# An encoder whose 1/rms row reaches the partitions through DRAM instead of through TensorE transposes

## The chip, the cores and the metric

The kernel runs on one core of a Trainium2 chip. The metric is the device time of one launch in microseconds (us); one launch computes the whole encoder. PE stands for the matrix engine, DVE, ACT and POOL for the vector, scalar and GpSimd engines, SP for the queue that starts most of the loads.

## The reference

The input x is 512 tokens by 1024 features, in fp32. There are two layers of this kind, and a final norm:

```python
for l in range(2):
    h = rms_norm(x, norm_g[l, 0])
    x = x + 0.5 * swiglu(h, ...)                    # 1024 -> 2816 -> 1024
    h = rms_norm(x, norm_g[l, 1])
    ya = neighbourhood_attention(h, ...)            # 8 heads of 64
    yb = diff_attention(h, ...)                     # 4 heads of 2 x 64, values of 128
    yc = window_gqa(h, ...)                         # 8 heads of 64
    g = sigmoid(h @ w_gate[l] + b_gate[l])          # a gate for each of the three branches
    x = x + (sum of g_i * (branch_i @ w_branch[l, i])) @ w_o[l]
    h = rms_norm(x, norm_g[l, 2])
    x = x + 0.5 * swiglu(h, ...)
return rms_norm(x, final_g)

def rms_norm(x, g):
    return x * lax.rsqrt(jnp.mean(x * x, axis=-1, keepdims=True) + EPS) * g
```

A differential head forms two softmax maps, takes one minus lambda times the other, multiplies the values by this, and then has an rms norm of its own over the 128 features of its output for each token. So each layer has three norms of x that go through the code in question, and four head norms: six and eight in the whole kernel. (The final norm is computed in another way.)

## The kernel before

**Tiling.** x is kept transposed: 8 tiles of 128 features (partitions) by 512 tokens. A product of the weights with h gives a tile of 128 output features by 512 tokens. fp32 precision comes from a split of both factors into a high and a low part; `product` (L97, L98, L100) issues 24 matmuls for one output tile where the inner size is 1024: for each of 8 chunks high by high and high by low, then 8 times low by high. The value projections (L492, L493, L495) have the tokens as output partitions instead. The weights come from DRAM once (`weights`: L82 a DMA on SP's queue, L83 a cast on ACT, L84 a subtraction on DVE).

**The norms.** The gain is folded into h; the factor 1/rms of each token is applied after the products. `sums` (through `rstd`) makes four small matmuls with a column of ones (L157, two records each in the trace), which give the sum of squares for 4 x 128 tokens as four columns in the PSUM tile `st`; DVE scales them and adds epsilon (L158), POOL raises them to -0.5 (L159). The result `rs` has tokens on partitions. The value products, whose outputs have tokens on partitions, use it as it is (`vn<-mm,rs`). Everything else needs one row of 512 factors repeated on all 128 partitions: `spread` (L165) makes four PE transposes of a broadcast column into `st`, and in `finish` ACT copies the tile to SBUF as `rb` (L150). The first user of `rb` is a DVE multiplication that reads a product in PSUM: `gn` (L296) in a feed-forward part, `qn` (L451) in a mixer. There are three PSUM buffers for products (`mm`), one for `st`, two for scores (`s`), one for transposed maps (`t`), one for a head's output (`av`).

**Where the six norms stand.** In a feed-forward part, `sums` comes behind the first product of the part and `finish` behind the second. In a mixer, `sums` comes behind the query product, `finish` behind the key product, and two value products of 24 half-width matmuls follow. The first feed-forward part of layer 0 (`opening`) runs four products at once while x and weights come in; its 32 low-part matmuls (L353) come last, with `sums` behind the 16th and `finish` behind the 24th.

**The differential heads.** `attend_diff` is a generator that gives its work in 8 pieces (two maps for each of four blocks of 128 queries); `beside` takes one piece, then issues some side products (gates, query and key products of later heads, merges), and what a piece leaves for later is issued one step (one piece) behind: scores and softmax (L533, L534, L544, L547), then the transposes of the map (L672 on PE, `ph` on ACT by L673, `pl` on DVE by L674), then the gather (L689), then for a whole head the sum of squares (`rstd_of`), then `scaled`: four transposes of the factors (L165 again), one DVE instruction that reads them from PSUM (L705), and the split of the head's output into `yp` (ACT L107, DVE L109), which the merges read much later. A head's norm thus falls into the first pieces of the next head. The third head's falls into the fourth, the fourth's into the first grouped-query pair.

**What sets the order.** The instructions of each engine are put in order by the tile framework's scheduler from its own estimates; on the chip each engine runs its list in order, and waits where something isn't there. POOL issues the DMAs that keep x in DRAM (`d_x`, L61), read it back (`x`, L56) and swap the halves of query tiles (`qks`, L464, L465), and in a mixer it forms the position bias tiles `nab` (L617).

Of the kernel before, what the change touches and what calls it, by code (L numbers as in the profile page):

```python
# [11 lines left out]
F32 = mybir.dt.float32  # L12
# [4 lines left out]
P = 128  # L17
# [16 lines left out]
def encoder(ctx: ExitStack, tc: tile.TileContext, a: dict, out: bass.AP):  # L34
# [77 lines left out]
    class Norm:  # L112
# [27 lines left out]
        def sums(self):  # L140
# [3 lines left out]
            rstd(self.acc, 1.0 / D, rt, self.rs)  # L144

        def finish(self):

            pb = spread(self.rs)
            rb = work.tile([P, S], F32, tag="rb", name="rb", bufs=1)
            nc.scalar.copy(rb, pb)  # L150
            self.rb = rb

# [7 lines left out]

    def spread(rs):

        pb = st_tile()
        for j in range(4):
            nc.tensor.transpose(pb[:, j * P : (j + 1) * P], rs[:, j : j + 1].to_broadcast([P, P]), ident)  # L165
        return pb

# [83 lines left out]
    def ffn(l, i, h, nxt=None):  # L251
        with tc.tile_pool(name="ffn", bufs=1) as fp:
# [5 lines left out]
            for m in range(2 if first else 0, MF):  # L258
                wg = weights(a["w_gu"][l, i, m, 0])
                wu = weights(a["w_gu"][l, i, m, 1])  # L260
                pg = mm_tile()
                product(pg, cols(wg, KC), h.hi, h.lo)
                if m == 0:
                    h.sums()
                pu = mm_tile()
                product(pu, cols(wu, KC), h.hi, h.lo)
                if m == 0:
                    h.finish()
                if m == 4 and first:
                    position_tables()  # L270
                    small_values()
                if nxt is None and 4 <= m < 4 + KC:
                    if m == 4:
                        xt = fp.tile([P, 4, D], F32, tag="xt", name="xt")
                    x_turned(xt, m - 4)
                gated(h, fp, pg, pu, ghi, glo)
# [28 lines left out]
    def opening(l, i, h, fp, ghi, glo):  # L305
# [42 lines left out]
        for k in range(KC):  # L348
            h.square(k, xs[k])
        for n in range(4):  # L350
            for k in range(KC):
                wk = slice(k * P, (k + 1) * P)
                nc.tensor.matmul(ps[n], ws[n][1][:, wk], h.hi[k], start=False, stop=k == KC - 1)  # L353
            if n == 1:
                h.sums()
            if n == 2:
                h.finish()
        gated(h, fp, ps[0], ps[1], ghi, glo)
# [71 lines left out]
    def mixer(l, h, nxt):  # L430
        with tc.tile_pool(name="mix", bufs=1) as mp:
# [36 lines left out]
            def qk(n):  # L468

                pq = projected(2 * n)  # L470
                if n == 0:
                    h.sums()
                    pk = projected(1)
                    h.finish()
                q = scaled_by(pq, -0.125)
# [183 lines left out]
            def attend_diff(head):  # L659
# [38 lines left out]
                def rstd_of(o, sq):  # L698
                    rt = small.tile([P, 8], F32, tag="rt", name="rt", bufs=3)
                    rstd(sq, 1.0 / P, rt, rt)  # L700
                    return lambda: scaled(o, rt)

                def scaled(o, rt):
                    pb = spread(rt)
                    nc.vector.scalar_tensor_tensor(out=o, in0=o, scalar=sg, in1=pb, op0=ALU.mult, op1=ALU.mult)  # L705
                    ys[1].append(split(o, mp, "yp", 12))
# [178 lines left out]
            beside(attend_diff(1), [g0(5)[0], merge(0, 2), qk(6), v_diff(1)], 6)  # L885
            beside(attend_diff(2), [*g0(6, 7), merge(0, 3), qk(7)], 5)
            beside(attend_diff(3), [gqa_keys(), gqa_queries(0), *g1(0, 1, 2)], 6)
            beside(attend_gqa(0), [*[gqa_queries(p) for p in (1, 2, 3)], merge(1, 0), *g1(3, 4)], 6)
            beside(attend_gqa(1), [merge(1, 1), *g1(5, 6), merge(1, 2), *g1(7)], 5)
            beside(attend_gqa(2), [merge(1, 3), *[gate(2, m, "v", 8) for m in range(3)]], 4)  # L890
# [112 lines left out]
```

## Time and profile before

| | |
|---|---|
| median of 3 runs | 2495.88 us (2495.48 to 2496.05) |
| the profiled execution's own time | 2496.59 us |
| its span | 2494.8 us |
| mean granted TensorE clock | 0.999 |
| PE busy | 2469.8 us |
| DVE, ACT, POOL busy | 1352.6, 983.4, 188.8 us |

The page of the profile covers one execution. Its rows give an engine's instruction group as "line, engine, operation, output from inputs, shape, count", with the busy time and the mean duration; a timeline row begins with the start in us from the start of the span and the duration in us, and ends, in brackets, with the idle time of the engine ahead of it and what ended that. The ends of matmuls are modelled: the spacing of their starts is a better measure than their duration.

### The profile page before, as it was taken

What the parts mean: (1) busy time and instruction counts of PE and PEld (TensorE: products, weight loads), DVE (VectorE), ACT (ScalarE), POOL (GpSimd) and SP (SyncE); (2) the same over time, 40 slices, a digit from 0 to 9 for tenths busy, and PEclk for the clock granted to TensorE, in tenths of its full rate; (3) what the DMA queues carried; (4) which work ended last, traced back from release to release, by engine and by line L of the source; (5) the groups of instructions that cost most, each with busy time, mean ns of one, the idle gap of its engine ahead of it and who ended that gap; (6) DMA issues with size and microseconds to landing.
All of it is one profiled execution on the core that took longest, in us unless ns stands there. A gap on an engine that the chain in (4) does not pass through costs nothing. (4 is left out here: it accounts for less than half of the span.)

```text
span 2494.8 us, 30423 instructions
## 1 busy us (share of the span) xinstructions
PE 2469.8 (99%) x11800; PEld 2059.5 (83%) x11800; DVE 1352.6 (54%) x2331; ACT 983.4 (39%) x1608; POOL 188.8 (8%) x287
## 2 busy tenths in 40 slices
PE   8999999999999999999999999999999999999998
PEld 6788888888888788888888888888888888888887
DVE  5444336876777644443344443377776777444432
ACT  4332224644555433332233332256445554333222
POOL 1000003311000000000000000032110001000000
PEclk9999999999999999999999999999999999999999
DMA  5333444432322342324433234443322224333232
GB/s 162 100 101 91 120 135 128 113 93 84 99 86 79 120 131 94 100 91 125 131 104 99 94 96 128 141 122 104 94 87 90 89 74 148 124 113 97 93 101 68
DMA packets 80271, 265.24 MB, mean 106 GB/s; under 512 B 10720, under 2 KB 15360, under 8 KB 80128
## 3 DMA queue, kind: packets, MB, share of 16 engines
q1 hardware_dynamic: 67968, 228.42, 29.7%
q0 software_dynamic: 11008, 33.03, 4.6%
q8 instruction: 93, 1.52, 0.3%
q10 hardware_dynamic: 1152, 1.86, 0.2%
q14 instruction: 50, 0.41, 0.1%
HBM read 241.22 MB, written 12.62 MB: 102 GB/s over the span
## 5 line engine op out<-in xcount | busy, mean ns | idle before, releaser
L97 PE MATMUL mm<-h,whi 128*128 128x512 f32 x2112 | 829.1, 393 | 0.0
L98 PE MATMUL mm<-l,whi 128*128 128x512 f32 x2112 | 826.4, 391 | 0.0
L83 ACT CAST whi<-raw 128x1024 fp32r<-128x1024 f32 (+1 forms) x414 | 430.4, 1042 | 782.6 <-PE mm L98 363.7
L84 DVE TENSOR_TENSOR wlo<-raw,whi 128x1024 fp32r<-128x1024 f32 (+1 forms) x414 | 499.6, 1207 | 285.2 <-ACT whi L83 158.7
L100 PE MATMUL mm<-h,wlo 128*128 128x512 f32 x2112 | 522.0, 389 | 0.0
L100 PEld LDWEIGHTS mm<-h,wlo 128*128 128x128 f32 x2112 | 396.3, 188 | 82.6
L97 PEld LDWEIGHTS mm<-h,whi 128*128 128x128 f32 x2112 | 396.8, 188 | 81.0 <-issue 2.2
L98 PEld LDWEIGHTS mm<-l,whi 128*128 128x128 f32 x2112 | 396.7, 188 | 79.0
L299 DVE TENSOR_TENSOR un<-mm,rb 128x512 f32<-128x512 f32 x87 | 60.1, 691 | 296.7 <-PE mm L100 296.7
L288 PE MATMUL mm<-g,whi 128*128 128x512 f32 x528 | 205.4, 389 | 0.0
L289 PE MATMUL mm<-g,whi 128*128 128x512 f32 x528 | 205.4, 389 | 0.0
L107 ACT CAST g<-un 128x512 fp32r<-128x512 f32 x88 | 54.7, 622 | 250.5 <-DVE un L300 250.5
L296 DVE TENSOR_TENSOR gn<-mm,rb 128x512 f32<-128x512 f32 x88 | 60.8, 691 | 133.6 <-PE mm L100 133.6
L291 PE MATMUL mm<-g,wlo 128*128 128x512 f32 x528 | 131.4, 389 | 0.0
L547 ACT ACTIVATE lg<-lg,negm 128x256 f32<-128x256 f32 (+1 forms) x192 | 114.6, 597 | 29.7 <-DVE negm L544 28.0
L61 POOL DMA_DIRECT2D d_x<-x x40 | 22.1, 553 | 1249.7 <-DVE x L247 1249.4
L288 PEld LDWEIGHTS mm<-g,whi 128*128 128x128 f32 x528 | 99.1, 188 | 20.6
L291 PEld LDWEIGHTS mm<-g,wlo 128*128 128x128 f32 x528 | 99.1, 188 | 20.6
L289 PEld LDWEIGHTS mm<-g,whi 128*128 128x128 f32 x528 | 99.1, 188 | 20.6
L297 ACT ACTIVATE gn<-gn 128x512 f32<-128x512 f32 x88 | 56.0, 636 | 123.9 <-DVE gn L296 123.9
L109 DVE TENSOR_TENSOR g<-un,g 128x512 fp32r<-128x512 f32 x88 | 60.9, 692 | 62.2 <-ACT g L107 62.2
L247 DVE SCALAR_TENSOR_TENSOR x<-mm,x 128x512 f32<-128x512 f32 x40 | 27.7, 692 | 109.5 <-PE mm L291 72.7
(214 smaller groups left out, 3048.2 us busy)
## 6 DMA issues: line engine op xcount, KB each, us to landing
raw<-in_w_gu SPq DMA_DIRECT2D x172, 512.0 KB, 3.5
raw<-in_w_down SPq DMA_DIRECT2D x48, 512.0 KB, 3.6
raw<-in_w_gate SPq DMA_DIRECT2D x48, 512.0 KB, 3.6
raw<-in_w_qk SPq DMA_DIRECT2D x44, 512.0 KB, 3.6
raw<-in_w_branch SPq DMA_DIRECT2D x24, 512.0 KB, 3.6
raw<-in_w_last SPq DMA_DIRECT2D x22, 512.0 KB, 3.5
d_x<-x POOLq DMA_DIRECT2D x40, 256.0 KB, 2.5
x<-d_x POOLq DMA_DIRECT2D x40, 256.0 KB, 2.9
```

What stands on the lines that cost most here:

```text
L83: nc.scalar.copy(hi[:, w], raw[:, w])
L84: nc.vector.tensor_tensor(out=lo[:, w], in0=raw[:, w], in1=f(hi[:, w]), op=ALU.subtract)
L97: nc.tensor.matmul(ps, wh, xhi[k], start=k == 0, stop=False)
L98: nc.tensor.matmul(ps, wh, xlo[k], start=False, stop=False)
L100: nc.tensor.matmul(ps, wl, xhi[k], start=False, stop=k == n - 1)
L109: nc.vector.tensor_tensor(out=lo, in0=src, in1=f(hi), op=ALU.subtract)
L288: nc.tensor.matmul(ps, w[k][0], ghi[c + k], start=c + k == 0, stop=False)
L289: nc.tensor.matmul(ps, w[k][0], glo[c + k], start=False, stop=False)
L291: nc.tensor.matmul(ps, w[k][1], ghi[c + k], start=False, stop=c + k == MF - 1)
L296: nc.vector.tensor_tensor(out=gn, in0=pg, in1=h.rb, op=ALU.mult)
L299: nc.vector.tensor_tensor(out=un, in0=pu, in1=h.rb, op=ALU.mult)
L547: nc.scalar.activation(p, p, AF.Exp, bias=negm, scale=-1.0, accum_out=total)
```

## The change

`spread` no longer uses PE. It writes the 4 x 128 factors as a row of 512 numbers to a tile in DRAM (a POOL DMA, 512 pieces of 4 bytes), and a second POOL DMA reads this row back to all 128 partitions (256 KB). `finish` is gone, and with it ACT's copy; for a norm of x the two DMAs stand directly behind POOL's power, and the tile that they fill is `rb`. In `opening`, `sums` stands ahead of the 32 low-part matmuls. For a differential head the row goes to a tile `rd` (one of the two `x` buffers), and `scaled` is issued one step later, by `after(1, ...)`, and reads `rd` from SBUF. Some side products stand beside another piece: the merge that stood beside the third head now stands beside the fourth, and the gates of the second branch move on by one.

```diff
@@ class Norm
             rstd(self.acc, 1.0 / D, rt, self.rs)
-        def finish(self):
-            pb = spread(self.rs)
-            rb = work.tile([P, S], F32, tag="rb", name="rb", bufs=1)
-            nc.scalar.copy(rb, pb)
-            self.rb = rb
+            self.rb = work.tile([P, S], F32, tag="rb", name="rb", bufs=1)
+            spread(self.rs, self.rb, f"d_r{self.step}")
...
-    def spread(rs):
-        pb = st_tile()
-        for j in range(4):
-            nc.tensor.transpose(pb[:, j * P : (j + 1) * P], rs[:, j : j + 1].to_broadcast([P, P]), ident)
-        return pb
+    def spread(rs, rb, name):
+        row = dram.tile([1, S], F32, tag=name, name="d_r")
+        nc.gpsimd.dma_start(at(row, 0, [[1, P], [P, 4]]), rs[:, :4])
+        nc.gpsimd.dma_start(rb, row.to_broadcast([P, S]))
@@ def ffn
                 product(pu, cols(wu, KC), h.hi, h.lo)
-                if m == 0:
-                    h.finish()
@@ def opening
             h.square(k, xs[k])
+        h.sums()
         for n in range(4):
             for k in range(KC):
                 wk = slice(k * P, (k + 1) * P)
                 nc.tensor.matmul(ps[n], ws[n][1][:, wk], h.hi[k], start=False, stop=k == KC - 1)
-            if n == 1:
-                h.sums()
-            if n == 2:
-                h.finish()
@@ def qk
                     pk = projected(1)
-                    h.finish()
@@ def attend_diff
                     rstd(sq, 1.0 / P, rt, rt)
-                    return lambda: scaled(o, rt)
-                def scaled(o, rt):
-                    pb = spread(rt)
+                    pb = work.tile([P, S], F32, tag="x", name="rd", bufs=2)
+                    spread(rt, pb, f"d_r{l}_{head}")
+                    return after(1, lambda: scaled(o, pb))
+                def scaled(o, pb):
                     nc.vector.scalar_tensor_tensor(out=o, in0=o, scalar=sg, in1=pb, op0=ALU.mult, op1=ALU.mult)
@@ the pieces and what is issued beside them
-            beside(attend_diff(2), [*g0(6, 7), merge(0, 3), qk(7)], 5)
-            beside(attend_diff(3), [gqa_keys(), gqa_queries(0), *g1(0, 1, 2)], 6)
-            beside(attend_gqa(0), [*[gqa_queries(p) for p in (1, 2, 3)], merge(1, 0), *g1(3, 4)], 6)
-            beside(attend_gqa(1), [merge(1, 1), *g1(5, 6), merge(1, 2), *g1(7)], 5)
+            beside(attend_diff(2), [*g0(6, 7), qk(7)], 4)
+            beside(attend_diff(3), [merge(0, 3), gqa_keys(), gqa_queries(0), *g1(0, 1)], 6)
+            beside(attend_gqa(0), [*g1(2), *[gqa_queries(p) for p in (1, 2, 3)], merge(1, 0), *g1(3)], 6)
+            beside(attend_gqa(1), [*g1(4), merge(1, 1), *g1(5, 6), merge(1, 2), *g1(7)], 6)
```

The scheduler puts the new instructions into each engine's list. Three places show what came of it.

POOL, at the start of layer 0's mixer, before (`nab` is a piece of position bias, `qks` a half of a swapped query tile):

```order
L61 DMA d_x<-x 128x512
L56 DMA x<-d_x 128x512
L159 TENSOR_TENSOR rs<-rt,nhalf 128x4
L617 TENSOR_TENSOR nab<-mask,rp 128x256 x6
L465 DMA qks<-qk 64x512
L464 DMA qks<-qk 64x512 x2
L465 DMA qks<-qk 64x512
```

and with the change, at the same place:

```order
L154 TENSOR_TENSOR rs<-rt,nhalf 128x4
L159 DMA d_r<-rs 128x4x1
L605 TENSOR_TENSOR nab<-mask,rp 128x256 x3
L160 DMA rb<-d_r 128x512
L605 TENSOR_TENSOR nab<-mask,rp 128x256 x3
L454 DMA qks<-qk 64x512
L453 DMA qks<-qk 64x512 x2
```

The write of the row follows the power at once; three of the six bias pieces stand between it and the issue of the read. Line numbers shift: the power is L159 before and L154 now, the bias L617 and L605.

DVE, where the norm of the second differential head ends, before (`o` is the head's output, `st` the transposed factors):

```order
L544 ISA lg_5140,negm_5080<-s_5137,dpb_5000 128x512
L544 ISA negm_5080 128x1
L705 SCALAR_TENSOR_TENSOR o_5076<-o_5076,sg_256,st_5147 128x512
L84 TENSOR_TENSOR wlo_5374<-raw_5372,whi_5373 128x1024
L730 RECIPROCAL tot_5081<-tot_5081 128x2
L109 TENSOR_TENSOR yp_5155<-o_5076,yp_5153 128x512
```

and with the change:

```order
L722 SCALAR_TENSOR_TENSOR lg_5078<-lg_5078,tot_5074,lg_5103 128x512
L694 SCALAR_TENSOR_TENSOR o_5034<-o_5034,sg_256,rd_5089 128x512
L440 SCALAR_TENSOR_TENSOR qn_5141<-mm_5116,rb_2667 128x512
L532 ISA lg_5162,negm_5157<-s_5159,dpb_4993 128x512
L532 ISA negm_5157 128x1
L109 TENSOR_TENSOR yp_5168<-o_5034,yp_5166 128x512
L448 TENSOR_TENSOR qk_5143<-qn_5141,qk_5143 64x512
L448 TENSOR_TENSOR qk_5146<-qn_5141,qk_5146 64x512
L662 TENSOR_TENSOR pl_4996<-t_5170,ph_4995 128x4x128
```

The scaling (L705 before, L694 now) stands one piece later, and behind it now stand the next softmax (L532) and the low part `pl` of the next transposed map, which the gather reads. On ACT the same place now reads (`yp` is the high part of the scaled output, `ph` that of the transposed map):

```order
L83 CAST whi_5391<-raw_5390 128x1024
L107 CAST yp_5166<-o_5034 128x512
L661 CAST ph_4995<-t_5170 128x4x128
L447 CAST qk_5143<-qn_5141 64x512
```

so that ACT takes the cast of the scaled output ahead of the map's.

DVE, for the third head, with the change:

```order
L694 SCALAR_TENSOR_TENSOR o_5386<-o_5386,sg_256,rd_5456 128x512
L440 SCALAR_TENSOR_TENSOR qn_5508<-mm_5483,rb_2667 128x64x8
L662 TENSOR_TENSOR pl_5303<-t_5460,ph_5302 128x4x128
L532 ISA lg_5523,negm_5518<-s_5520,dpb_5300 128x512
L532 ISA negm_5518 128x1
```

Here the low part of a map (L662) stands behind the scaling too; PE writes the next map into the same PSUM buffer `t` only after it.

## The prediction

> **What bounds the kernel now.** I read the shares of busy time first, then the costliest groups:
>
> ```profile
> PE 2469.8 (99%) x11800; PEld 2059.5 (83%) x11800; DVE 1352.6 (54%) x2331; ACT 983.4 (39%) x1608; POOL 188.8 (8%) x287
> L97 PE MATMUL mm<-h,whi 128*128 128x512 f32 x2112 | 829.1, 393 | 0.0
> ```
>
> PE is busy for 2469.8 of 2494.8 us, and its largest group had 0.0 us of idle time ahead of it. So only two things can move the time: PE instructions that go, and PE idle time that goes or comes. The other engines count where PE waits for them. The transposes that go, with what PE waited for ahead of them:
>
> ```profile
> L165 PE MATMUL st<-ident,rt x32: 271/272/323, 579.5 to 1935.4; 128*128 128x128 f32 x32
> L165 PE MATMUL st<-ident,rs x24: 270/272/306, 34.6 to 2134.8; 128*128 128x128 f32 x24
>   POOL rt L159: 8.8, 12
> ```
>
> These are 8 groups of four for heads (`rt`) and 6 for norms (`rs`). What a group costs is read from the starts around it in the timeline, for the second head of layer 0, which didn't wait, and for the other three:
>
> ```profile
> 28.24 3.79 PE L353 MATMUL mm<-h,wlo 128*128 128x512 f32 x16
> ...
> 578.47 0.39 PE L97 MATMUL mm<-h,whi 128*128 128x512 f32 x1
> 579.50 0.65 PE L165 MATMUL st<-ident,rt 128*128 128x128 f32 x4 [0.64 <-POOL rt L159]
> 579.91 0.48 PE L98 MATMUL mm<-l,whi 128*128 128x512 f32 x1
> ...
> 619.26 0.39 PE L534 MATMUL s<-qk,qks 128*128 128x512 f32 x1
> 619.48 0.60 PE L165 MATMUL st<-ident,rt 128*128 128x128 f32 x4
> 619.84 0.48 PE L97 MATMUL mm<-h,whi 128*128 128x512 f32 x1
> 620.16 0.40 PE L98 MATMUL mm<-l,whi 128*128 128x512 f32 x1
> ...
> 659.62 0.65 PE L165 MATMUL st<-ident,rt 128*128 128x128 f32 x4 [0.73 <-POOL rt L159]
> ...
> 702.10 0.65 PE L165 MATMUL st<-ident,rt 128*128 128x128 f32 x4 [0.18 <-POOL rt L159]
> ```
>
> Matmuls of this width start (3.79 - 0.39) / 15 = 0.2275 us apart (the first row, from the opening). The second head's group moved the next matmul from 619.49 to 619.84, and the one behind it by 0.09 more (0.32 instead of 0.23): 0.45 us. The first head's: 579.91 - 578.47 - 0.23 = 1.21, and 0.09 makes 1.30, or the bracket plus 0.66. By that rule the third costs 1.39 and the fourth 0.84. **Removed** from PE: 1.30 + 0.45 + 1.39 + 0.84 = 4.0 us in a layer, 8.0 in two, and 6 x 0.45 = 2.7 at the norms.
>
> **The new path.** Behind POOL's power now stand two DMAs, one after the other. The nearest rows:
>
> ```profile
> d_x<-x POOLq DMA_DIRECT2D x40, 256.0 KB, 2.5
> x<-d_x POOLq DMA_DIRECT2D x40, 256.0 KB, 2.9
> d_gqa<-tg POOLq DMA_DIRECT2D x1, 16.0 KB, 1.7
> POOL x L56 <- DMA d_x<-x: 96.7, 35, 4.4
> L61 POOL DMA_DIRECT2D d_x<-x x40 | 22.1, 553 | 1249.7 <-DVE x L247 1249.4
> q0 software_dynamic: 11008, 33.03, 4.6%
> ```
>
> A POOL DMA issue takes 0.55 us (553 ns). The kernel has this very pattern already, a write to DRAM and a read of it: POOL waited 96.7 / 35 = 2.76 us behind the issue of the write, so 3.3 us from start to start. I take 3.55 for the 512 pieces of 4 bytes, a quarter more for the many pieces (my choice). The read is like `x<-d_x`, 256 KB to 128 partitions: 0.55 + 2.9 = 3.45. Together 7.0 us from the end of the power to `rb` or `rd`, where a group of transposes took 0.45 us and a copy. Lower bound: both like `d_gqa`, 0.55 + 1.7, with the 0.25 by which the wait of 2.76 is longer than the 2.5 of the row: 2.5 each, 5.0. Upper bound: a piece costs what a packet of that queue takes, 0.046 x 2494.8 x 16 / 11008 = 0.167 us; 512 pieces on 16 engines are 32 x 0.167 = 5.3 us, with 0.55 and `d_gqa`'s 1.7 some 7.5, and 11.0 with the read.
>
> [...]
>
> **The opening.** Rows of before:
>
> ```profile
> 31.87 0.95 PE L157 MATMUL st<-ones,acc 128*128 128x1 f32 x8
> ...
> 33.51 1.04 POOL L159 TENSOR_TENSOR rs<-rt,nhalf 128x4 f32<-128x4 f32 x1 [22.59 <-DVE rt L158]
> ...
> 36.02 0.68 DVE L296 TENSOR_TENSOR gn<-mm,rb 128x512 f32<-128x512 f32 x1
> ...
> 36.94 0.39 PE L97 MATMUL mm<-h,whi 128*128 128x512 f32 x1
> ```
>
> The sums stood at 31.87, 3.63 us behind the first low-part matmul at 28.24, and now stand at 28.24, so the power ends at 34.55 - 3.63 = 30.9, `rb` is there at 37.9, `gn` ends at 38.6. All four product buffers are taken, so the next product can start only then, at 38.7 and not at 36.94: **+1.75**. PE has run out of low-part matmuls by 28.24 + 0.8 + 32 x 0.2275 = 36.3.
>
> **The mixers.** Three of six bias pieces stand on POOL between the two DMAs.
>
> ```profile
> 384.90 1.05 POOL L159 TENSOR_TENSOR rs<-rt,nhalf 128x4 f32<-128x4 f32 x1 [1.85 <-DVE rt L158]
> 388.71 3.21 POOL L617 TENSOR_TENSOR nab<-mask,rp 128x256 f32<-128x256 f32 x3 [2.77 <-DMA rp<-in_na_rpb]
> 391.22 1.28 DVE L451 SCALAR_TENSOR_TENSOR qn<-mm,rb 128x512 f32<-128x512 f32 x2
> 392.96 0.28 PE L492 MATMUL mm<-whi,h 128*128 128x256 f32 x1
> ...
> 1621.92 3.24 POOL L617 TENSOR_TENSOR nab<-mask,rp 128x256 f32<-128x256 f32 x3 [3.02 <-DMA raw<-in_w_v]
> 1625.88 0.28 PE L492 MATMUL mm<-whi,h 128*128 128x256 f32 x1
> ```
>
> The first bias piece waits for its table until 388.71, and three take 3.21. So the read is issued at 391.92, though the row is there by 385.95 + 3.55 = 389.5. `rb` comes at 391.92 + 3.45 = 395.4, `qn` 0.7 later. The query, key and first value products hold the three `mm` buffers; the second value product needs the query's, so it starts at 396.2 instead of 392.96: **+3.25**. In layer 1: 1625.16 + 3.45 + 0.7 + 0.1 = 1629.45 instead of 1625.88: **+3.6**. Both include the transposes that go. A quicker write doesn't shorten these two.
>
> **The other feed-forward parts.** There `gn` frees a buffer for the fourth product. The worst of the three is the last:
>
> ```profile
> 2128.07 0.94 PE L157 MATMUL st<-ones,acc 128*128 128x1 f32 x8
> ...
> 2130.42 1.03 POOL L159 TENSOR_TENSOR rs<-rt,nhalf 128x4 f32<-128x4 f32 x1
> ```
>
> The power ends 3.4 us behind the sums' start, `rb` follows at 10.4, `gn` ends at 11.1. PE needs the buffer 0.94 + 2 x 24 x 0.2275 = 11.85 behind the same start. So two whole products hide it (by 0.75 us here, one for one beyond that; I price the other two by this one), and what stays is **3 x -0.45 = -1.35**.
>
> **The heads.** Layer 0's second and third:
>
> ```profile
> 613.33 0.95 PE L157 MATMUL st<-ones,sqd 128*128 128x1 f32 x8
> 614.56 1.45 POOL L159 TENSOR_TENSOR rt<-rt,nhalf 128x4 f32<-128x4 f32 x1 [12.18 <-DVE rt L158]
> ...
> 656.50 0.94 PE L157 MATMUL st<-ones,sqd 128*128 128x1 f32 x8
> 657.98 1.58 POOL L159 TENSOR_TENSOR rt<-rt,nhalf 128x4 f32<-128x4 f32 x1 [10.63 <-DVE rt L158]
> ```
>
> I count from the start of the sums. Second head: the power ends at +2.7, `rd` is there at +9.7, DVE scales it by +10.45, ACT's cast of it ends at +11.1 (0.61) and only then casts the next map's `ph`, by +11.65. PE reaches the gather that needs that map after the sums (0.95), two groups of transposes (0.45 each), three pairs of scores (0.46 each), a product of 24 (5.46) and two matmuls, at +9.15: it idles **2.5**. Third head: power +3.06, `rd` +10.06, scaled +10.8, `qn` (1.05) +11.85, `pl` (0.7) +12.55; PE wants to overwrite the map's PSUM buffer after the sums, two groups, two pairs of scores, a product and five matmuls, at +9.35: **3.2**. The first head is just in time (0.1), since 48 value matmuls stand ahead of its gather; at the fourth, a merge needs the scaled output itself some 0.65 us before it is there, and smaller waits make about 1.2. Nothing covers these because PE takes its instructions in order. 7.0 us a layer, against the 4.0 that go. The moved side products should also save this wait, some 0.5 us a layer:
>
> ```profile
> 644.82 0.63 PE L672 MATMUL t<-ident,lg 128*128 128x128 f32 x4 [0.45 <-DVE lg L733]
> ```
>
> In sum 7.0 - 4.0 - 0.5 = 2.5, times two layers: **+5.0**. `rd` shares its two buffers with `x`; no x is loaded between the heads, so I cost that at nothing.
>
> **The clock.** In the opening a gap was followed by a slow stretch (columns: window, us, PE busy, clock, DMA share, GB/s):
>
> ```profile
> 14.00:17.50 3.50, 1.40 (x6) 1.00 1.00 377
> 17.50:21.20 3.70, 3.70 (x10) 0.54 0.80 319
> ```
>
> PE was idle for 2.1 of 3.5 us, and the next 3.7 ran at 0.54, which loses 3.7 x 0.46 = 1.7 us. Four of the new stalls are 3.2 us or longer (two mixers, two third heads); I take two of them to be followed by such a stretch: **+3.4**. If every one were, +6.8.
>
> [...]
>
> **The sum:** 1.75 + 6.85 - 1.35 + 5.0 + 3.4 = +15.65 on the profiled execution's 2496.6 us (1.8 more than its span), so 2512.3; the median of 2495.88 lies 0.7 below that execution: **2512 us**, rounded.
>
> **Rivals.** (1) *The pair is quick; not slower than before.* It decides from about 5 us downward. At 4.5 us the second head's 2.5 is gone and 0.7 is left of the third's 3.2: -4.0 - 0.5 + 0.7 = -3.8 a layer; the opening is bound by PE at 36.3, -0.65; the other parts -1.35; the mixers keep 6.85 - 2 x 0.95, since only a quicker read helps them; no stall is long enough for the clock. -7.6 - 0.65 - 1.35 + 4.95 = -4.65: 2491. For it: 1.7 us for a small write. Against it: 2.9 for a read of 256 KB. If no wait came in the transposes' place at all, -8.0 - 2.7 - 1.0 = -11.7: 2484; POOL's order at the mixers speaks against that. (2) *The pieces are slow.* At 11.0 us the opening gains 4, the mixers 1.5 each, the three parts 3.25 each, the eight heads about 3.95 each: 12.25 (the sum without the clock) + 4 + 3 + 9.75 + 31.5 = 60.5, with five slow stretches 69: 2565. At 8.5 us: opening 1.5, heads 12, the parts 2.25, four slow stretches 6.8: 12.25 + 22.55 = 34.8, so 2531. (3) *The clock falls at every stall over 2 us:* about 8 stretches in place of 2, 10 us more: 2522.
>
> **How the numbers follow.** No change means within 0.2%, 5 us, about what a measurement of this kernel can tell. The forecast, with rival 3 in it and the latency from 5.5 to 8.5 us, has 0.66, and its own range is 2499 to 2531 (at 5.5 the heads lose 4.2 us a layer less, the opening 1.5, the mixers 0.75 each and one slow stretch 1.7: 2512 - 13 = 2499). The quick pair, 2487 to 2496, has 0.17, nothing waiting (2484) 0.07, slow pieces of over 8.5 us 0.10. Half of the quick pair lies beyond -5: faster 0.07 + 0.07 = 0.14. The rest of it and a sliver of the forecast's low end make the same 0.13, and 0.73 is left for slower. The range, 2490 to 2532, leaves out 2484, the quickest pairs and most of the slow pieces, some 0.19.
>
> **What would show it.** Right: the read of the row at the mixers is issued behind the third bias piece, and PE idles 3 to 4 us ahead of the second value product; the write lands in 2.5 to 4 us; PE idles 2 to 3.5 us at the second and third head of each layer, with ACT `ph` or DVE `pl` named as releaser; no wait in the last feed-forward part. Wrong: a pair well under 5 us, or over 9; PE's idle time growing without PE's clock, or the other way about; a wait elsewhere, as for `x` buffers.

## The result, and the profile after

The changed kernel takes 2639.12 us (median of 5 runs, 2636.57 to 2641.85) against 2495.88 before: 1.0575 times as long, interval 1.0564 to 1.0587. That is 143 us more, where 16 were forecast; the direction was right, the size was far outside the range.

The page of the changed kernel, from its busy times and its chain of work:

```profile
PE 2498.5 (95%) x11744; PEld 2080.2 (79%) x11744; DVE 1354.8 (51%) x2331; ACT 977.8 (37%) x1602; POOL 205.3 (8%) x315
...
PE 78%; issue 12%; DMA 5%; DVE 2%; POOL 1%; ACT 1%; POOLq 0%; DVEq 0%; ACTq 0%
```

The span grew from 2494.8 to 2637.3 us, by 142.5. PE's idle time grew from 2494.8 - 2469.8 = 25.0 to 138.8 us, and PE's busy time from 2469.8 to 2498.5, though it runs 56 fewer matmul records. So there are two losses: 113.8 us of idle, and 28.7 us of busy time, which must be slower matmuls. The view of PE's waits (engine, tile and line, what it waited for: us in total, times, the longest) says where the idle time is:

```profile
PE mm L97 <- DVE gn L288: 29.3, 4, 11.0
PE av L677 <- ACT ph L661: 20.6, 2, 10.3
PE t L660 <- DVE pl L662: 20.4, 2, 10.6
PE mm L97 <- ACT yp L107: 19.4, 4, 9.3
PE mm L480 <- DVE qn L440: 16.2, 2, 8.5
PE av L677 <- DVE pl L662: 14.4, 2, 7.7
```

They are 14 stalls of 5.9 to 11.0 us, one for each of the 6 norms and 8 heads, 118.9 us together (19.4 counts two small ones of 0.75 us too, that were there before). Behind them stand the two DMAs of the new path (output from input, queue, count, KB each, median us from issue to landing):

```profile
d_x<-x POOLq DMA_DIRECT2D x40, 256.0 KB, 2.5
...
rd<-d_r POOLq DMA_DIRECT2D x8, 256.0 KB, 4.1
...
rb<-d_r POOLq DMA_DIRECT2D x6, 256.0 KB, 4.2
...
d_r<-rt POOLq DMA_DIRECT2D x8, 2.0 KB, 9.9
d_r<-rs POOLq DMA_DIRECT2D x6, 2.0 KB, 9.4
```

Here a write of 2 KB takes four times as long as one of 256 KB, 9.9 us against 2.5. The landing of a row counts from the start of the issue. The timeline of the second head, for which the prediction counted from the sums at +0 (here 642.86):

```profile
642.86 0.83 PE L152 MATMUL st<-ones,sqd 128*128 128x1 f32 x7
...
644.10 1.04 POOL L154 TENSOR_TENSOR rt<-rt,nhalf 128x4 f32<-128x4 f32 x1 [11.25 <-DVE rt L153]
645.69 0.82 POOL L159 DMA_DIRECT2D d_r<-rt  x1 [0.56 <-POOL rt L154]
651.69 0.40 PE L98 MATMUL mm<-l,whi 128*128 128x512 f32 x1
655.88 0.56 POOL L160 DMA_DIRECT2D rd<-d_r  x1 [9.37 <-DMA d_r<-rt]
660.37 0.75 DVE L694 SCALAR_TENSOR_TENSOR o<-o,sg,rd 128x512 f32<-128x512 f32 x1 [11.54 <-DMA rd<-d_r]
661.16 0.62 ACT L107 CAST yp<-o 128x512 fp32r<-128x512 f32 x1 [11.57 <-DVE o L694]
661.68 0.58 ACT L661 CAST ph<-t 128x512 fp32r<-128x512 f32 x1
662.31 0.58 PE L677 MATMUL av<-ph,vd 128*128 128x256 f32 x1 [10.23 <-ACT ph L661]
```

PE ran out of work at 652.1, that is +9.2, as forecast (+9.15); the order of DVE and ACT made it wait for the scaling, as forecast; but `rd` was there at 660.4, +17.5, and not at +9.7. From the end of the power at 645.14 it is 15.2 us instead of 7.0 (13.7 to 16.2 over the 14 places).

The second loss is the clock. The opening's stall, and what follows it (window, us, PE busy, clock, DMA share, GB/s):

```profile
40.00:46.70 6.70, 0.00 (x0) 0.50 0.47 152
46.70:52.10 5.40, 5.37 (x13) 0.50 0.18 49
```

The clock is down to half while PE is idle, and stays there for 5.4 us after work has begun again: 2.7 us lost. All 14 stalls show this: the clock fell 1.9 to 5.1 us after PE had stopped, and 3.1 to 6.0 us of half clock were left after the restart, 72.3 us in sum, so 36 us lost. The account: +118.9 of stalls, +36 of clock, less some 11 that the forecast counts as removed: 144, against the 142.5 us measured.

### The profile page after: what moved, and what is told of

Same layout as the page of the kernel before. It is cut to its first block, busy times and chain, and to the rows that moved or that the text cites. A ratio compares the mean times of both kernels' runs of the same rounds, so it can differ in the third digit from the quotient of the medians.

```text
span 2637.3 us, 30339 instructions
## 1 busy us (share of the span) xinstructions
PE 2498.5 (95%) x11744; PEld 2080.2 (79%) x11744; DVE 1354.8 (51%) x2331; ACT 977.8 (37%) x1602; POOL 205.3 (8%) x315
## 4 chain that ended last, share of the span: by engine, by line
PE 78%; issue 12%; DMA 5%; DVE 2%; POOL 1%; ACT 1%; POOLq 0%; DVEq 0%; ACTq 0%
PE mm L97 18%; PE mm L98 17%; PE mm L100 17%; PE mm L281 5%; PE mm L283 5%; PE mm L280 5%; DMA d_r<-rt 2%; DMA d_r<-rs 1%; PE av L576 1%; PE t L566 1%; PE mm L480 1%; PE mm L481 1%; DMA rb<-d_r 1%; DMA rd<-d_r 1%; PE mm L483 1%
## 5 line engine op out<-in xcount | busy, mean ns | idle before, releaser
L97 PE MATMUL mm<-h,whi 128*128 128x512 f32 x2112 | 839.9, 398 | 29.3 <-DVE gn L288 29.3
L98 PE MATMUL mm<-l,whi 128*128 128x512 f32 x2112 | 836.0, 396 | 0.0
L97 PEld LDWEIGHTS mm<-h,whi 128*128 128x128 f32 x2112 | 403.3, 191 | 113.9 <-DVE gn L288 19.6
L98 PEld LDWEIGHTS mm<-l,whi 128*128 128x128 f32 x2112 | 403.6, 191 | 81.4
L97 PE MATMUL mm<-yp,whi 128*128 128x512 f32 x192 | 76.4, 405 | 19.4 <-ACT yp L107 19.4
## 6 DMA issues: line engine op xcount, KB each, us to landing
raw<-in_w_gu SPq DMA_DIRECT2D x172, 512.0 KB, 3.5
raw<-in_w_down SPq DMA_DIRECT2D x48, 512.0 KB, 3.6
raw<-in_w_gate SPq DMA_DIRECT2D x48, 512.0 KB, 3.6
raw<-in_w_qk SPq DMA_DIRECT2D x44, 512.0 KB, 3.6
raw<-in_w_branch SPq DMA_DIRECT2D x24, 512.0 KB, 3.6
raw<-in_w_last SPq DMA_DIRECT2D x22, 512.0 KB, 3.4
```

The source lines that it names most:

```text
L97: nc.tensor.matmul(ps, wh, xhi[k], start=k == 0, stop=False)
L98: nc.tensor.matmul(ps, wh, xlo[k], start=False, stop=False)
```

## Experiments

**What makes the write slow.** The kernel before, with one write behind each head scaling that nothing reads; layouts and queues differ. Of the edit two of eight:

```diff
+                    if n == 0:
+                        nc.gpsimd.dma_start(at(row, 0, [[1, P], [P, 4]]), rt[:, :4])
+                    if n == 2:
+                        nc.gpsimd.dma_start(at(row, 0, [[16, P], [16 * P, 4]]), rt[:, :4])
```

> The kernel before, with one unused write to DRAM behind each of the eight head scalings, so that only its landing time is measured: layer 0, head by head, POOL's queue: 512 pieces of 4 bytes side by side as in the change; the same 512 factors as 128 pieces of 16 bytes; 512 pieces of 4 bytes, 64 bytes apart; 128 pieces of 4 bytes. Layer 1: the 512 pieces from SP's queue; the 128 pieces of 16 bytes from SP's queue; 256 pieces of 4 bytes on POOL's; 8 pieces of 2 KB on POOL's. Theory (the number of pieces sets the write): 512 pieces land in 9 to 10 us wherever they lie and whoever issues them, 256 in about 6, both kinds of 128 in about 4, 8 in 1.8. Rival 1 (neighbouring small pieces get in each other's way in memory): the spaced 512 land in under 4 us. Rival 2 (POOL prepares each piece): the 512 from SP land in under 4 us. The whole stays within 5 us of 2496.

It took 2495.57 us, as before. The landing times, one write each (the lines are those of the eight writes; the answers for the first and third):

```profile
L713 POOL DMA_DIRECT2D d_p<-rt x1: 820/820/820, 578.2 to 578.2; - x1
DMA to landing us min/median/max: 10.3/10.3/10.3
...
L717 POOL DMA_DIRECT2D d_p<-rt x1: 825/825/825, 658.3 to 658.3; - x1
DMA to landing us min/median/max: 2.3/2.3/2.3
```

The theory fell. The same 512 pieces of 4 bytes land in 10.3 us where they lie side by side and in 2.3 where they lie 64 bytes apart. 128 pieces side by side take 9.5, nearly as long as 512; 256 in four rows of 64 take 8.3; 128 pieces of 16 bytes take 2.7, 8 pieces of 2 KB 1.9. From SP's queue the 512 take 9.1 and the 128 of 16 bytes 2.1, so it isn't POOL's preparation either. The four slow ones, 8.3 to 10.3 us, are those whose pieces of 4 bytes lie side by side.

Nor does the trace show the DMA engines at work on the pieces for so long. While the first write was under way, issued at 578.21 and landed at 588.55, they had long stopped (window, us, POOL busy, clock, DMA share, GB/s):

```profile
578.20:580.30 2.10, 0.82 (x1) 1.00 0.66 219
580.30:584.00 3.70, 0.00 (x0) 1.00 0.00 0
```

The trace's packets of this write end 2.1 us behind the start of its issue, and the landing is told 8.3 us later. In the changed kernel all 14 writes are like this: the packets end after 1.8 to 3.7 us, the landing follows 6.0 to 8.2 us behind them. So a count or a price of packets doesn't show this cost here. A second kernel of this kind asked how near:

> The kernel before with one unused write to DRAM behind each head scaling, all from POOL's queue, to see which neighbours get in each other's way. Layer 0: 512 pieces of 4 bytes, 8 bytes apart; 16 bytes apart; 32 bytes apart; 16 pieces of 4 bytes side by side (64 bytes in all). Layer 1: 32 such pieces (128 bytes); 64 pieces of 32 bytes side by side; 32 pieces of 64 bytes side by side; 64 pieces of 4 bytes (256 bytes). Theory 1 (the pieces that share 64 bytes are written one after the other): the 16 side by side take 8 us or more already, 8 bytes apart about 6, 16 apart 3 to 4, 32 apart and pieces of 32 or 64 bytes about 2.3. Theory 2 (pieces in a wider stretch, some 512 bytes, wait for each other): 16 pieces take 3 us or less, 32 about 4, 64 about 6, and 512 pieces 8 bytes apart still 8 or more.

| written | apart | landing |
|---|---|---|
| 512 x 4 bytes | 4 bytes (side by side) | 10.3 us |
| 512 x 4 bytes | 8 bytes | 4.4 us |
| 512 x 4 bytes | 16 bytes | 3.1 us |
| 512 x 4 bytes | 32 bytes | 2.3 us |
| 512 x 4 bytes | 64 bytes | 2.3 us |
| 128 x 4 bytes | side by side | 9.5 us |
| 64 x 4 bytes | side by side | 6.3 us |
| 32 x 4 bytes | side by side | 4.3 us |
| 16 x 4 bytes | side by side | 2.0 us |
| 64 x 32 bytes | side by side | 1.7 us |

The first theory fell: 16 neighbours within 64 bytes landed in 2.0 us, no later than pieces 32 or 64 bytes apart (2.3). The second had 16, 32 and 64 right (2.0, 4.3, 6.3 against 3, 4 and 6), but not 512 pieces 8 bytes apart (4.4, not 8). With more neighbours the landing came later: 2.0, 4.3, 6.3 and 9.5 us for 16, 32, 64 and 128 pieces, and 10.3 for 512. Why isn't shown: behind the last packet the trace has nothing of the write but its landing. And these are single landings: the same write of 128 pieces of 16 bytes landed in 1.7 to 3.9 us in the 14 places of a later kernel, so differences of one or two us in this table mean little by themselves. Counted from the end of the last packet, the 16, 32, 64 and 128 neighbours took 0.5, 2.1, 4.5 and 8.0 us, so their order stands. One more write, 32 pieces of 64 bytes, took 5.1 us, but it was issued 0.6 us behind another at a busy moment: its packets ended only 4.2 us after its issue, and it landed 0.9 us behind them.

**Do the parts add?** Heads alone, and norms alone:

```diff
 (heads by DRAM, norms as before)
-            self.rb = work.tile([P, S], F32, tag="rb", name="rb", bufs=1)
-            spread(self.rs, self.rb, f"d_r{self.step}")
+        def finish(self):
+            pb = turned_rows(self.rs)
...
 (norms by DRAM, heads by transposes)
-                    spread(rt, pb, f"d_r{l}_{head}")
-                    return after(1, lambda: scaled(o, pb))
+                    return after(1, lambda: scaled(o, rt))
-                def scaled(o, pb):
+                def scaled(o, rt):
+                    pb = turned_rows(rt)
```

> The change with the six norms of x taken back to transposes; the eight heads stay with the row in DRAM, and the side products stay moved. Theory (each norm pays its own stall and its own slow stretch of the clock, and the parts add): the heads' eight stalls in the changed kernel sum to 73.4 us, the half-clock stretches behind them cost 21, and about 9 us of transposes and waits are gone: 2496 + 85 = 2581, 2573 to 2590. Rival (the loss comes from something common, such as the moved side products or the shared x buffers): over 2600 here, or under 2560.

> The change with the eight heads taken back to transposes, issued one step later than before, and the side products moved; the six norms of x keep the row in DRAM. Theory: the six stalls of the changed kernel sum to 45.5 us, the slow stretches behind them cost 15, 2.7 us of transposes are gone, and the heads save about 5 by no longer waiting for POOL: 2496 + 53 = 2549, 2541 to 2557. Rival (common cause): over 2570 or under 2530.

Heads alone: 2575.84 us against 2494.89 on that chip, 1.0324 (1.0294 to 1.0354), 81 us more. Norms alone: 2547.29, 1.0209 (1.018 to 1.0239), 52 us more. Both lie inside their expectations, and together they are 133 of the 143 us. So most of the loss has no common cause: each place pays for its own stall and its own clock. Of the 10 us that are missing, 4.6 are stalls that were a little shorter here (70.4 and 43.9 us, against 73.4 and 45.5 in the changed kernel), and some 4 the half clock behind them (64.8 us instead of 72.3).

**The clock by itself.** Useless matmuls on PE behind each sum of squares, so that they take the place of most of the stall:

```diff
             spread(self.rs, self.rb, f"d_r{self.step}")
+            fill(self, {0: 36, 1: 28, 4: 28}.get(self.step, 22))
...
+    def fill(h, n):
+        ps = st_tile()
+        for j in range(n):
+            nc.tensor.matmul(ps, h.hi[0][:, 0:P], h.hi[j % KC], start=j == 0, stop=j == n - 1)
```

> The changed kernel with useless matmuls of 128x512 on PE behind each of the 14 sums of squares, 22 to 36 of them, 5 to 8.2 us, a little less than the stall that follows there, so that each stall is cut to 3 us or less. Theory (the stalls cost 119 us and, apart from that, the half clock behind them some 36): the idle time only changes places with useless work, but the clock stays up nearly everywhere: 2639 - 30 = 2609, 2600 to 2618. Rival 1 (the slow clock costs nothing on top): 2639. Rival 2 (the useless matmuls delay the chain itself): over 2645.

2631.56 us (2628.29 to 2634.84): some 8 us less than the changed kernel, outside the expected range, and with two runs 6.5 us apart hardly clear of noise; what follows rests on the trace. The clock did rise, from 0.971 to 0.992. The 414 useless matmuls take 94 us at 0.2275 each and the stalls shrank by 89, so that side cost 5; half clock after stalls fell from 72 us to 34, which is worth 19. The net gain of 14 is 3 us more than the spans show (2626.5 against 2637.3). What I had missed is how short a stall may be. The second head's gather in this kernel, with a stall of 3.09 us in the first of these windows, the restart in the second, and in the last a stretch behind a stall of 1.16 us at another place:

```profile
654.50:658.20 3.70, 0.70 (x4) 1.00 0.16 35
658.30:661.60 3.30, 3.30 (x13) 0.61 0.89 264
661.60:664.60 3.00, 3.00 (x16) 0.86 0.07 25
407.80:411.00 3.20, 3.20 (x27) 1.00 0.63 146
```

Here the clock was still full during the stall and fell after work had begun again; so it was at four of the nine places, and at the others it fell before the stall was over. In this kernel every stall of 2.3 us or longer, and two pairs of 1.3 to 1.7 us with 0.4 us of work between them, were followed by half clock, for 2.9 to 5.7 us of work, and those of 1.2 us were not. It is no sharp bound: in the kernel that comes next one stall of 2.7 us, in the opening, was followed by none.

**Does the sum hold with a quick write?** The row written as 128 pieces of 16 bytes; the users read the copied row through a permuted view:

```diff
-        nc.gpsimd.dma_start(at(row, 0, [[1, P], [P, 4]]), rs[:, :4])
+        nc.gpsimd.dma_start(at(row, 0, [[4, P], [1, 4]]), rs[:, :4])
...
-        nc.vector.tensor_tensor(out=gn, in0=pg, in1=h.rb, op=ALU.mult)
+        nc.vector.tensor_tensor(out=tok(gn), in0=tok(pg), in1=mixed(h.rb), op=ALU.mult)
```

> The changed kernel with the row stored so that each partition writes its four factors as one piece of 16 bytes (128 pieces side by side instead of 512 of 4 bytes); the multiplications read the copied row through a permuted view, so the result is the same. Theory (the write's 9.8 us is the whole difference to the forecast, and the forecast's sum holds with the right latency): the write lands in 2.7 us as measured alone, the path from the power to the copied row is 8.7 us instead of 15.6; stalls of about 4.1 us in the opening, 3.7 and 3.6 at the mixers, 18 at the heads, none in the other feed-forward parts, in all 30 instead of 119; eight of them are long enough for the clock, 16 us; 12 us of transposes, waits and the moved products' wait gone: 2496 + 34 = 2530, 2518 to 2542. Rival (the stalls have another cause, such as the read of one row by 128 partitions or the queue): over 2590.

2535.72 us, 1.0162 (1.0143 to 1.018), inside the expected range (2530, 2518 to 2542): another layout of 2 KB, with the reads that go with it, gives back 103 us. The write landed in 2.4 and 2.9 us (medians of norms and heads; 1.7 to 3.9 singly), and the path from power to row took 6.3 to 9.2 us, around the forecast's 7.0 (9.7 and 10.3 at the mixers, where the bias pieces stand between):

```profile
d_r<-rt POOLq DMA_DIRECT2D x8, 2.0 KB, 2.9
...
d_r<-rs POOLq DMA_DIRECT2D x6, 2.0 KB, 2.4
...
PE mm L494 <- DVE qn L454: 9.0, 2, 4.8
...
PE mm L97 <- DVE qk L462: 4.3, 2, 2.5
PE mm L97 <- DVE gn L294: 2.7, 1, 2.7
```

The mixers idle 4.2 and 4.8 us (3.7 and 3.6 expected), the opening 2.7 (4.1), the heads 8.0 (18 expected), the other feed-forward parts not at all; five stalls, not eight, were followed by half clock, 18.5 us of it behind the restarts, so 9 us lost. The permuted view has a price of its own: DVE's multiplications took 1.05 us instead of 0.69, and PE waited 4.3 us for `qk`, which it did neither before nor in the changed kernel. So the total came out near its expectation with parts that did not: with the forecast's 11 us for what was removed these figures make 22 of the 38 us by which the span grew, and where the other 16 lie wasn't looked into.

**Can something be kept?** The moved side products alone, and with the scaling one step later but with transposes:

```diff
-                    return lambda: scaled(o, rt)
+                    return after(1, lambda: scaled(o, rt))
```

> The kernel before with the moved side products alone. Theory: one wait of 0.5 us in each layer goes, 2495, faster by 1 us and no more than 2. Rival (the moved products cost, for example by a later merge): 1 to 5 us slower.

> The kernel before with the moved side products and with each head scaled one step later, the four transposes kept and issued at that later step. Theory: PE no longer waits for POOL's power ahead of the heads' transposes, 2.2 us a layer, and 0.5 by the moved products: 5.4 us less, 2490.5, 2488 to 2493. Rival (the waits only move to the softmax or to the merge): within 2 us of before.

The side products alone: 2494.36 us, 0.9995 (0.9986 to 1.0003), no difference that can be told. With the later scaling: 2492.28, 0.9990 (0.9981 to 0.9999), 2.7 us less, half of the 5.4 expected; PE's wait for POOL's power (3.1 us before) is gone. A third try, without transposes or DRAM:

```diff
+        nc.tensor.matmul(ps, allones, sq, start=True, stop=True)
+        nc.vector.tensor_scalar(rd, ps, scale, EPS, op0=ALU.mult, op1=ALU.add)
+        nc.gpsimd.tensor_tensor(out=rd, in0=rd, in1=nhalf[:, 0:1].to_broadcast([P, S]), op=ALU.pow)
```

> As the kernel before it, but a head's sum of squares is formed by one fp32 matmul of a 128x128 tile of ones with the 128x512 squares, which leaves the sums on all partitions at once; DVE scales 128x512, POOL takes the power of 128x512, and neither transposes nor DRAM are used for the heads. Theory (the matmul takes four passes of 0.23 us, 0.9 in all, against 0.95 for the sums and 0.45 for the transposes): 4 us less than with the transposes one step later, 2487, 2484 to 2490. Rival (POOL's power of 512 columns is slow, and the scaled output and what DVE has behind it come late): 2495 or more.

3140.83 us. No run shows the four passes that the theory counted; in the kernel before, an fp32 matmul with 512 columns stands as two records (L190), of 0.59 us each and 1.02 together, so their starts lie 0.43 us apart; that makes an estimated 0.86 us, near the theory's 0.9:

```profile
69.70 1.02 PE L190 MATMUL st<-hot,tab 32*4 32x512 f32 x2
```

The rival won by far; the power of 512 columns, its exponent read as one repeated column, takes 82.6 us where that of 4 took 1.0 to 2.2:

```profile
L169 POOL TENSOR_TENSOR rd<-rd,nhalf 128x512 f32<-128x512 f32 x8 | 660.5, 82561 | 112.9 <-DVE rd L168 112.9
```

**Is the latency harmless where it is hidden?** First three heads of each layer: the row through DRAM as in the change, the scaling issued five pieces behind the sums; the fourth head and the norms by transposes:

```diff
+                    if head == 3:
+                        return after(1, lambda: scaled(o, turned_rows(rt)))
+                    row = put(rt, f"d_r{l}_{head}")
+                    return after(1, lambda: fetched(o, row))
+                def fetched(o, row):
+                    pb = work.tile([P, S], F32, tag="x", name="rd", bufs=2)
+                    nc.gpsimd.dma_start(pb, row.to_broadcast([P, S]))
+                    return after(2, lambda: scaled(o, pb))
```

> The moved side products; the first three heads of each layer get their row through DRAM as in the change, but the read is issued two pieces behind the write and the scaling three pieces behind that, some 25 us behind the power; the fourth head, whose output is needed soon, and the norms of x use transposes. Theory (the 15 us of the path cost nothing where enough pieces lie between): no stall at the first three heads, six groups of transposes and their waits less than before: 2490, 2487 to 2493. Rival (POOL, which waits 10 us for the write, holds up the swaps of query tiles behind it, or the long life of the buffers delays something): 2496 or more.

2548.94 us, 1.0213 (1.0198 to 1.0227): a time that the rival allowed (2496 or more), but by the mechanism of neither. The stalls at the second and third heads were as long as in the change:

```profile
PE t L677 <- DVE pl L679: 20.2, 2, 10.6
PE av L694 <- ACT ph L678: 19.9, 2, 10.3
```

The engines' lists say why. The scaling was written several pieces later in the program, but the scheduler, which goes by its own estimate of when the row is there, put it on DVE where the change has it. DVE of this kernel at the second head:

```order
L745 SCALAR_TENSOR_TENSOR lg<-lg,tot 128x512
L717 SCALAR_TENSOR_TENSOR o<-o,sg,rd 128x512
L456 SCALAR_TENSOR_TENSOR qn<-mm,rb 128x512
L549 ISA lg,negm<-s,dpb 128x512
L549 ISA negm 128x1
L679 TENSOR_TENSOR pl<-t,ph 128x4x128
```

So the place was then forced by data: the scaling's factor gets the row minimum of the softmax beside which the scaling is issued, times zero, added to it, and the read's target is first written with the row minimum of the softmax beside which the read is issued.

```diff
+                    nc.vector.tensor_copy(pb[:, 0:1], latest[0])
                     nc.gpsimd.dma_start(pb, row.to_broadcast([P, S]))
...
+                        nc.vector.scalar_tensor_tensor(
+                            out=by, in0=latest[0], scalar=0.0, in1=sg, op0=ALU.mult, op1=ALU.add
+                        )
```

> The kernel before this one put the late scaling into the program five pieces behind the sums, but the scheduler moved it back, ahead of the next map's low part, since by its own estimate the row is there early. Here the first three heads' read of the row and their scaling are tied by a data dependence to the softmax of the piece beside which they are issued (the scaling's factor gets that softmax's row minimum times zero added), so that they stand some 10 and 25 us behind the power on their engines. Theory (the 15 us of the path cost nothing where no engine's list reaches the waiting instruction early): the four stalls of 9.6 to 10.6 us and the two of 3.1 and 3.7 are gone, with the slow clock behind them; 2490, 2487 to 2494. Rival (POOL's wait for the write holds up the swaps of query tiles, and PE waits for these): 2500 or more.

2499.97 us, 1.0026 (1.0016 to 1.0036). All the stalls named were gone, 49 us less than the kernel before it, with the write as slow as ever, and POOL's queue held nothing up that PE waited for; but it was 6 us slower than the kernel before the change. The two mixers, from sums to sums in the timeline, were 2.1 us shorter than before (509.9 and 509.8 against 512.0 and 511.9). The loss lay in the down projections, where nothing is different: 126.4 us instead of 125.1 in each of three, from their first matmul to the next sums, and 123.4 instead of 119.8 for those of the last part, some 7 us in all. The largest group of matmuls before, and here:

```profile
L288 PE MATMUL mm<-g,whi 128*128 128x512 f32 x528 | 205.4, 389 | 0.0
```

```profile
L293 PE MATMUL mm<-g,whi 128*128 128x512 f32 x528 | 206.8, 392 | 0.0
```

The kernel had one new tile, of 4 bytes a partition twice, in a pool that lies ahead of the large tiles. Put into the place of a tile that exists, with every engine's list the same:

```diff
-                        by = small.tile([P, 1], F32, tag="by", name="by", bufs=2)
+                        by = small.tile([P, 1], F32, tag="se", name="by")
```

> The kernel before this one lost its four long stalls and its mixers became 2.1 us shorter than before, but the down projections of its feed-forward parts, whose instructions are the same in every kernel here, took 126.4 us instead of 125.1 each. It had one new tile of 8 bytes a partition ahead of the large tiles. Here that tile takes the place of one that exists, and every engine's list is the same. Theory (the new tile moved the others in SBUF, and the slower matmuls come from where their operands lie): the down projections take 125.1 again, and with 1.3 us less in three of them and some 3 us in the last part the time is 2492.6, 2491 to 2494.5. Rival (the slower down projections come from the work itself): 2500 again.

2490.66 us against 2494.90, 0.9984 (0.9975 to 0.9993): the lowest time of all, 4.2 us under the kernel before. The row is that of before again, and the last part's projections take 119.8 us again:

```profile
L293 PE MATMUL mm<-g,whi 128*128 128x512 f32 x528 | 205.4, 389 | 0.0
```

So in this kernel DRAM carried the factors of six heads without a loss (0.9984), with the same slow write, where no engine's list reached the user of the row before the row was there. That DRAM itself gains isn't shown: transposes one step later gave 0.9990 (0.9981 to 0.9999), and the two intervals overlap.

## Why the prediction was wrong

- **The latency of the new path: wrong, and the step that failed.** The prediction priced the write by the row of `d_x`, 3.55 us, and took "a piece costs what a packet of that queue takes" for the upper bound, 7.5. Measured: the issue stands 0.53 us behind the power (left out), takes 0.81 us instead of 0.55, and the write lands 8.9 to 10.9 us after the start of its issue. The read took 4.1 instead of 2.9 us, though it moves the same 256 KB; whether that comes from all partitions reading one row wasn't tried. (The forecast's 3.45 for the read adds the issue to a row that already holds it; by the row it is 2.9, so this slip made the forecast a little longer, and hid part of the error.) From the power to the row 15.2 us instead of 7.0, beyond the "upper" bound of 11.0. That bound gave each piece the time of a packet of that queue, 3 KB on average (33.03 MB in 11008), and the time that counted came behind the last packet, 6.0 to 8.2 us of it. The second rival had the right name, slow pieces, at a chance of 0.10, but its prices, 8.5 and 11.0 us for the pair, were too short as well. The first rival's 4.5 us for the pair lies below the forecast's own lower bound of 5.0, and no row or run shows it: the shortest path measured, with 16-byte pieces, took 6.3.
- **Where the stalls fall: right for the opening, the heads and the mixers.** PE ran dry where forecast: the second head at +9.2, with ACT's `ph` as releaser, the third with DVE's `pl`, the fourth at the merge's `yp`, the mixers at the second value product, the opening at `gn`. With 15.2 us for 7.0, 8.2 more, the forecast's own terms give 10.6 for the opening's stall of 2.4, from 36.3 to 38.7 (10.97 measured), 10.7 and 11.4 for the second and third heads' 2.5 and 3.2 (10.23 and 9.86), 8.3 and 9.4 for the others' 0.1 and 1.2 (7.69 and 9.35). The sum as a whole isn't borne out at the latency for which it was made: with 16-byte pieces, whose path was near it, the time was 2535.7 us and not 2512, though the permuted reads and five slow stretches instead of two are in that time too.
- **The mixers: the wrong wait.** The stalls were 7.75 and 8.46 us, where +3.25 and +3.6 were forecast. "A quicker write doesn't shorten these two" held only if the row was there first. It wasn't: POOL had done with the three bias pieces at 404.33 and waited 4.02 us more for the write,

```profile
408.34 0.58 POOL L160 DMA_DIRECT2D rb<-d_r  x1 [4.02 <-DMA d_r<-rs]
```

  so the order of POOL's list, on which the prediction put 6.85 us, was not what counted in the changed kernel. With the quick write of the 16-byte pieces the read was issued behind the bias pieces without a wait, and the stalls of 4.2 and 4.8 us are near the forecast's, 3.7 and 4.05 with the 0.45 of the transposes that no longer fill PE.
- **The other feed-forward parts: wrong by the same step.** The cover of two products was there, 0.75 us too long for 7.0 us of latency; at 15.2 three stalls of 5.9 to 6.4 came through (8.2 less 0.75 would be 7.45). With the quick write these parts took 0.47 to 0.49 us less than before, as the -0.45 each had it.
- **The clock: right that stalls are followed by half clock, size off.** Forecast 3.4 us for two stretches of 1.7. There were 14, and behind stalls of 6 to 11 us they cost 2.6 each, 36 us. The third rival, that every stall over 2 us is followed by one, is close to what the runs showed, though not its price of 1.7 for each. That none of the first rival's stalls, 2.3 and 2.65 us at the mixers among them, would be long enough for the clock was the author's estimate. In the runs stalls of 2.3 to 3.2 us were mostly enough, and in the changed kernel the clock fell as early as 1.9 us after PE had stopped.
- **What was removed: about half.** The two edits that only take waits away gained 2.7 us where their expectation counted 5.4. The 0.45 for a group of transposes that nothing waits for is borne out at the three norms above; for the heads no run separates it. One working is off: (3.79 - 0.39) / 15 is 0.2267, not 0.2275, which changes no term by more than 0.05 us.

## What to carry to other kernels

Price a transfer by the layout that it writes, not by its bytes, its packets or its queue: here 2 KB in 4-byte neighbours took longer than 256 KB in rows (9.9 against 2.5 us), and storing four factors together gave back 103 of the 143 us. A later place in the program is a wish where a scheduler sets the order from its own estimates: look at the engines' lists, and tie the instruction to later data where it must stand late. And where PE is full, as in this kernel, look at the clock behind a stall too: most stalls of over 2 us were followed by a stretch at half clock, and in the changed kernel that cost 36 us beside the 118.9 of the stalls.

## What the hardware showed that was not expected

- Small writes to neighbouring addresses, by single landings: 2.0, 4.3, 6.3 and 9.5 us for 16, 32, 64 and 128 pieces of 4 bytes side by side, 2.3 for 512 of them 32 or 64 bytes apart. The packets of the 512 side by side end 2.1 us after the start of the issue; the other 8.3 us pass before the landing is told.
- The stretches at half clock have few lengths, counted from the fall of the clock: one of 3.41 us in the trace of the kernel before, in the opening, and behind the changed kernel's 14 stalls two of 6.83, nine of 10.24 and three of 13.65 us, so two, three and four times 3.41.
- POOL's power took 82.6 us for 128x512 and 1.0 for 128x4, so by these two an estimated (82.6 - 1.0) / 508 = 0.16 us for each column.
- A new tile of 8 bytes a partition made the matmuls of the down projections 0.7% slower (392 instead of 389 ns), those of the last part 1.8% (396), and with it the kernel some 9 us slower, though every engine's list was the same (2499.97 against 2490.66). Where the operands then lay, and which of them counts, wasn't looked into.
